# A fourth cache buffer, and the last pair's attention output read from SBUF, in one step of a hybrid decoder layer

## The chip, the cores and the metric

The kernel runs on one core of one Trainium2 chip. The metric is the device time of one execution in microseconds. Before the change it was 1331.47 us, the median of three runs from 1330.33 to 1339.6 us.

The core has TensorE (PE; its weight loads are shown as PEld), VectorE (DVE), ScalarE (ACT), GpSimd (POOL) and SyncE (SP). Here SP does nothing but issue DMAs; each engine works through its own instructions in the order in which they were placed, and so does SP: a DMA whose wait isn't over holds up all DMAs behind it.

## The reference

One layer of a decoder on 1024 prompt tokens and 8 x 8 sample tokens, all in float32, with a model width of 1024. Of the second part, the feed-forward network, only the beginning is near the change.

```
h = rms_norm(x, norm_mix_g)
a_val, a_gate, q, k, v = split(h @ w_in)                 # 256, 256, 768, 768, 768 columns
a = silu(layer_norm(depthwise_conv(a_val * sigmoid(a_gate))))
o = attend(q, k, v)                                      # 12 heads of 64
x = x + concat(a, o) @ w_out                             # 1024 x 1024
h = rms_norm(x, norm_ffn_g)
g = depthwise_conv(h @ w_ffn_gate)
x = x + (silu(g) * (h @ w_ffn_up)) @ w_ffn_down
y = rms_norm(x, norm_final_g)
```

Each of the 12 heads merges three dilated windows (128 neighbours at stride 1, 512 at 4, 2048 at 16). The sample tokens attend to their own cache (cache_k_win, cache_v_win) as well as to the new tokens.

## The kernel before

**Layout.** Prompt and sample tokens stand side by side as N = 1088 columns; channels are on the 128 partitions. Heads are worked in six pairs, one pair filling 128 partitions. Every matrix product is made from split operands: a float32 value becomes a high part (a copy by ScalarE to float32r) and a low part (a subtraction on VectorE or GpSimd), and three matmuls add high x high, high x low and low x high in PSUM.

**Stages.** First come the input projections. For pairs 0 to 2 the sample attention follows at once, in a zone of SBUF called S. In the next stage (zone P on the right) the prompt attention of earlier pairs runs beside the projections of pairs 3 to 5. Then, from about 380 us, prompt attention of the later pairs (zone P), sample attention of pairs 3 to 5 (zone U) and the output projection (operands in zone G) run together until 559 us. The output projection is cut along its inner dimension into three parts of 3, 3 and 2 tiles of 128 rows: tiles 0 and 1 are the convolution, tiles 2 to 7 the six pairs. The attention and convolution outputs travel through DRAM tensors mixed[0] to mixed[7]. The first two parts are done by out_part (matmuls at L188 to L190, evictions to x2 at L887 to L891). The last part, with mixed[6] and mixed[7], that is pairs 4 and 5, opens the next zone F and is worked in halves of 544 columns by out_half (matmuls at L942 to L945, evictions at L1165), whose result goes into the norm and on into the feed-forward products.

**The cache.** A sample attention of a pair loads four key tiles and four value tiles of 768 KB each (load_cache, L172). They rotate through SBUFS[Z][0] buffers: four in zone S, three in zone U. The scores of one chunk are made from two key tiles (L566), the outputs of one group from two value tiles (L592). The tiles of scores, turned weights and outputs (sy, spt, so) of a pair share a tag "S" with three buffers.

**The residual input.** In the second part, for each of eight row blocks, a block of the input x is loaded (xr, L882) and added to x2 by GpSimd (L883); only then may VectorE add the projection (L887). The first of these loads is issued behind a given cache load, cached[8 * NS1 + X2], that is the 23rd of the 24 cache loads of zone U.

**The last pair's way.** normalise multiplies the turned denominators into the output of a pair, in two blocks u of 512 columns (the cat tiles, L780), and stores each to mixed[2 + p] (L783). The 64 sample columns come from sample_attention (osm, L606). load_input(i, h, tag) then loads one half h of mixed[6 + i] and splits it (L1003 the load, L1006 the high part, L1007 the low part on VectorE).

**Order.** A planner places each engine's instructions from the dependences, the program's order, priorities and its own estimate of times; it is run when the kernel is built. issue_after(ins) adds only order: what its block traces on the engine of ins is placed behind ins. The loads of the last part and of the next stage are chained in this way through last_load, the high parts on ScalarE through last_high. In out_half the first eviction is placed behind lows_made[-1], the low part that was traced last:

```
earlier = rooted[0] if h and j == 1 else residuals[-1] if residuals else lows_made[-1]
with tc.issue_after(earlier):
    residuals.append(nc.vector.tensor_add(x, all_of(ps), x).ins)
```

The products of out_half rotate through four pairs of PSUM banks. The zones reuse memory: zone F begins where zone G began, and reaches over U into P, and a tile of F may be written when the tiles that lay there have been read for the last time. Weights rotate through five tiles of 4 KB (tag "W").

Of the kernel before, what the change touches and what calls it, by code (L numbers as in the profile page):

```python
# [50 lines left out]
KB, VB, QB, YB, HB, UB, PT = 4, 2, 2, 9, 8, 2, 2  # L51
DCOPY = ((2,), (2,))
AHEAD = 4000
SBUFS = {"S": (4, 3, 2), "U": (3, 3, 1)}
NS1, PN = 3, 4
HEADS = (0, 5, 8)
SHEADS = (0,10,11)
# [8 lines left out]
RING, SQS = 5, 16  # L66
FIRST = (0, 1, 2, 4, 5)
BANKS = (3, 1, 0, 2)
X2 = 22
ONACT = (0,)  # L70
HN = N // 2
HF = NF // 2
# [12 lines left out]
def trunk_kernel(tc, xT, w_in, w_first, w_out, w_gate, w_up, w_down, par, kc, vc, sa, sf, pmask, smask,  # L85
                 yT, kT, vT, ca, cas, cf):
    nc = tc.nc
    with (
# [34 lines left out]
        def zt(z, tag, bufs, s, w=N, dt=F32):  # L123
            return zone[z].tile([P, w], dt, tag=tag, name=nm(s), bufs=bufs)
# [406 lines left out]

        def sample_attention(p, Z, masks):
            mask, z = masks
            SB, PB = SBUFS[Z][1:]
            _, new, vn = spill[p]

            za, zg = z[:, :P], [z[:, (1 + g) * P:(2 + g) * P] for g in range(2)]
# [7 lines left out]
                    nc.vector.tensor_copy(zg[g][r, :].rearrange("p (j c) -> p j c", c=32)[:, :, o:o + T],  # L545
                                          src.rearrange("p (j g t) -> p g j t", g=2, t=T)[:, g])
            st = sp.tile([P, 4], F32, tag="sst", name=nm("sst"), bufs=2)
            y = zt(Z, "S", SB, "sy", 7 * P)
            nc.gpsimd.memset(y[:, NKEY:], 0.0)
            for c in range(NCH):  # L550
                ps = bank(Z, "ss", PB)
# [18 lines left out]
                                               scalar=(st[:, 0:1] if c else 3e38), accum_out=st[:, c:c + 1])  # L570
            nc.scalar.activation(y[:, :NKEY], y[:, :NKEY], AF.Exp, bias=st[:, 1:2], scale=-1.0, accum_out=st[:, 2:3])
            nc.vector.reciprocal(st[:, 3:4], st[:, 2:3])
            pT = zt(Z, "S", SB, "spt", 7 * P)
            for k0, nk in ((0, 4), (4, 3)):
                pt = bank(Z, "ss", PB)
                for k in range(nk):
                    nc.tensor.transpose(pt[:, k * P:(k + 1) * P], y[:, (k0 + k) * P:(k0 + k + 1) * P], ident)
                nc.scalar.activation(pT[:, k0 * P:(k0 + nk) * P], pt[:, :nk * P], AF.Copy)
            o2 = zt(Z, "S", SB, "so", 2 * P)
            for g in range(2):  # L580
                po = bank(Z, "ss", PB)
                tiles = [load_cache(Z, vc[p, g, c]) for c in range(NCH)]
# [185 lines left out]
        def normalise(p, den, un):  # L768
            r = exchange(den[:, 0], den[:, 1], 4)
            dn = tiny("dn", 16).rearrange("p (n k) -> p n k", k=4)  # L770
            nc.vector.tensor_add(dn, r[:, 0], den[:, 1])
            nc.vector.reciprocal(dn, dn)
            for u in range(2):
                db = zt("P", "H", HB, "db", 512).rearrange("p (k h d) -> p k h d", k=4, h=2)
                nc.vector.tensor_copy(db, dn[:, u::2].rearrange("p h k -> p k h")[:, :, :, None].to_broadcast([P, 4, 2, 64]))
                rt = bank("P", "t", PT)
                for c in range(4):
                    nc.tensor.transpose(rt[:, c * P:c * P + P], db[:, c].rearrange("p h d -> p (h d)"), ident)
                c = zt("P", "H", HB, "cat", 512)
                last_cat[0] = nc.vector.tensor_mul(c.rearrange("p (j c) -> p c j", c=4),  # L780
                                                   rt.rearrange("p (c j) -> p c j", c=4),
                                                   un[u].rearrange("p (c j) -> p c j", c=4)).ins
                nc.sync.dma_start(mixed[2 + p][:, u * 512:u * 512 + 512], c)  # L783

        before = []

        def prompt_heads(i0, i1):

# [122 lines left out]
        out_part(*part)  # L911
        for n in PARTS[1:-1]:
            out_part(*load_part(n, staged, g_part))
        zu.__exit__(None, None, None)
        zg.__exit__(None, None, None)
        zp.__exit__(None, None, None)
# [82 lines left out]
        def load_input(i, h, tag):  # L999
            nonlocal last_load, last_high  # L1000
            raw = slot("b11", "mx", F32)
            with tc.issue_after(last_load):
                last_load = nc.sync.dma_start(raw, mixed[k0 + i][:, h * HN:h * HN + HN]).ins  # L1003
            hi, lo = early[tag].pop() if early[tag] else slot(tag, "mh"), slot(tag, "ml")
            with tc.issue_after(last_high):
                last_high = nc.scalar.activation(hi, raw, AF.Copy).ins  # L1006
            lows_made.append(nc.vector.tensor_sub(lo, raw, hi.bitcast(F32)).ins)  # L1007
            part[h].append((hi, lo))

        def split_halves(t):  # L1010
# [9 lines left out]
        for h, tag in enumerate(("b11", "t2")):  # L1020
            load_input(0, h, tag)
            if not h:
                raw_wd = {m: slot("b22", "wr", F32, n1 * P) for m in ORDER[:DEFER]}
            for m0 in ORDER[h * 4:h * 4 + 4:2]:
                raw = slot("t1", "wr", F32, 2 * n * P)
                queued(raw.rearrange("p (m c) -> p m c", m=2), w_out[m0:m0 + 2, :, k0 * P:].rearrange("m p c -> p m c"))
                if m0 == ORDER[h * 4]:
                    load_input(1, h, tag)
                hi, lo = early["b21"].pop() if early["b21"] else slot("b21", "wh", w=512), slot("b21", "wl", w=512)
                with tc.issue_after(last_high):  # L1030
                    last_high = parts_of(raw, hi, lo)
                hi, lo = [t.rearrange("p (k c) -> p k c", c=P) for t in (hi, lo)]
                for j in range(2):
                    wl[m0 + j] = hi[:, j * n:j * n + n], lo[:, j * n:j * n + n]
# [6 lines left out]
        for i in range(n1):  # L1041
            hi, lo = slot("t3", "mh"), slot("t3", "ml")
            raw = lo.bitcast(F32)
            queued(raw, mixed[kd + i][:, HN:])
            with tc.issue_after(last_high):
                last_high = parts_of(raw, hi, lo)
            highs.append(last_high)
            deferred.append((hi, lo))
        for m in ORDER[:DEFER]:
            hi, lo = [slot("b22", t, w=n1 * P) for t in ("wh", "wl")]  # L1050
            with tc.issue_after(last_high):
# [701 lines left out]
```

## Time and profile before

| | |
|---|---|
| median of three runs | 1331.47 us |
| the profiled execution | 1330.07 us |
| its span | 1328.3 us |
| TensorE busy | 1291.3 us, 97% |
| VectorE, ScalarE, GpSimd busy | 941.7, 561.4, 468.9 us |
| TensorE idle, 380 to 440 us | 4.4 us |
| TensorE idle, 440 to 520 us | 6.2 us |
| HBM read and written | 153.97 MB and 56.04 MB |

The span is from the first to the last instruction of the profiled execution; its time has 1.8 us around that. A line of the profile names the engine, the line of the code (L783), the operation and the program's names as out<-in. A wait names who waited for whom. The granted clock is the share of TensorE's full clock that it was given.

### The profile page before, as it was taken

To read this page: it belongs to the slowest core of one execution; us is meant where nothing else is said; L and a number is where in the kernel's file an instruction comes from. 1 tells how busy PE (TensorE), PEld (TensorE's weight loads), DVE (VectorE), ACT (ScalarE), POOL (GpSimd) and SP (SyncE) were. 2 spreads that over 40 slices of the span, in tenths; PEclk is the share of its full clock that TensorE was granted. 3 is DMA by queue.
4 is the path that set the end of the run, shared out by engine and by line. 5 is a ranking of instruction groups with operands and counts; after the bars stand their busy time and mean duration, and the time that the engine had idled before them with its cause. 6 is when DMAs were issued, how large, how long until landed. Compare 5 with 4: busy or idle time off the path is not lost.

```text
span 1328.3 us, 25992 instructions
## 1 busy us (share of the span) xinstructions
PE 1291.3 (97%) x10322; PEld 1249.9 (94%) x10322; DVE 941.7 (71%) x1795; ACT 561.4 (42%) x1129; POOL 468.9 (35%) x384
## 2 busy tenths in 40 slices
PE   9999999999999999999999999999999999999996
PEld 9999998998978787899999999999999999999996
DVE  7479879555675666689976767667776569967656
ACT  7322121547585475355533323333233444334532
POOL 0121112111101104431765645656465535444600
PEclk9999999999999999999999999999999999999998
DMA  8247777565779879460113322133222394352412
GB/s 311 71 151 292 266 255 192 179 168 137 221 253 258 251 228 300 142 234 26 50 74 123 123 91 98 58 123 110 104 72 83 116 380 157 108 191 83 156 41 96
DMA packets 93801, 211.70 MB, mean 159 GB/s; under 512 B 13936, under 2 KB 42736, under 8 KB 93680
## 3 DMA queue, kind: packets, MB, share of 16 engines
q1 hardware_dynamic: 93392, 209.82, 48.1%
q8 instruction: 81, 1.33, 0.4%
q14 instruction: 40, 0.33, 0.1%
q10 hardware_dynamic: 288, 0.22, 0.1%
HBM read 153.97 MB, written 56.04 MB: 158 GB/s over the span
## 4 chain that ended last, share of the span: by engine, by line
PE 77%; DVE 13%; DMA 7%; issue 1%; ACT 1%; SPq 0%; DVEq 0%; ACTq 0%
PE g L188 6%; PE g L190 6%; PE g L189 6%; PE py L942 4%; PE py L944 4%; PE py L945 4%; PE g L942 4%; PE g L945 4%; PE g L944 4%; PE pz L944 3%; PE pz L942 3%; PE pz L945 3%; PE px L942 3%; PE px L945 3%; PE px L944 3%; PE o L762 3%
## 5 line engine op out<-in xcount | busy, mean ns | idle before, releaser
L188 PE MATMUL g<-xh,wh 128*128 128x384 f32 (+1 forms) x472 | 156.8, 332 | 1.6 <-DVE qkv L465 0.9
L163 POOL TENSOR_TENSOR wl<-wr,wh 128x1024 fp32r<-128x1024 f32 (+1 forms) x34 | 59.8, 1759 | 278.9 <-PE g L190 168.0
L190 PE MATMUL g<-xh,wl 128*128 128x384 f32 (+1 forms) x472 | 155.3, 329 | 0.0
L189 PE MATMUL g<-xl,wh 128*128 128x384 f32 (+1 forms) x472 | 155.2, 329 | 0.0
L942 PE MATMUL g<-ux,as 128*128 128x272 f32 x504 | 145.1, 288 | 2.3 <-DVE x L1575 1.4
L945 PE MATMUL g<-ux,as 128*128 128x272 f32 x504 | 145.4, 288 | 0.0
L944 PE MATMUL g<-ux,as 128*128 128x272 f32 x504 | 144.7, 287 | 0.0
L1093 POOL TENSOR_TENSOR wb<-wr,wb 128x512 fp32r<-128x512 f32 x79 | 116.1, 1481 | 50.2 <-ACT wb L1092 50.2
L1485 POOL TENSOR_TENSOR as<-ar,as 128x640 fp32r<-128x640 f32 (+1 forms) x56 | 89.6, 1612 | 105.9 <-ACT as L1484 105.9
L1092 ACT ACTIVATE wb<-wr 128x512 fp32r<-128x512 f32 x79 | 49.7, 629 | 162.9 <-DVE wr L1127 104.4
L942 PEld LDWEIGHTS g<-ux,as 128*128 128x128 f32 x504 | 95.0, 189 | 2.7 <-ACT as L1484 2.7
L945 PEld LDWEIGHTS g<-ux,as 128*128 128x128 f32 x504 | 94.8, 188 | 0.0
L944 PEld LDWEIGHTS g<-ux,as 128*128 128x128 f32 x504 | 94.6, 188 | 0.0
L1093 POOL TENSOR_TENSOR wa<-wr,wa 128x512 fp32r<-128x512 f32 x40 | 62.6, 1567 | 90.6 <-ACT wa L1092 86.7
L1353 DVE SCALAR_TENSOR_TENSOR fc<-gb,prm,fc 128x1104 f32<-128x1104 f32 x44 | 82.5, 1896 | 14.7 <-ACT fc L1351 14.4
L188 PEld LDWEIGHTS g<-xh,wh 128*128 128x128 f32 x472 | 88.7, 188 | 4.0 <-issue 2.0
L714 ACT ACTIVATE y<-y,m 128x128 f32<-128x128 f32 (+1 forms) x192 | 88.5, 464 | 7.9 <-DVE m L702 7.7
L189 PEld LDWEIGHTS g<-xl,wh 128*128 128x128 f32 x472 | 88.8, 188 | 0.2
L190 PEld LDWEIGHTS g<-xh,wl 128*128 128x128 f32 x472 | 88.8, 188 | 0.0
L415 DVE SCALAR_TENSOR_TENSOR cacc<-gp,prm,cacc 128x1024 f32<-128x1024 f32 x60 | 84.3, 1404 | 0.1
L677 DVE CUSTOM_DVE_ANT_0 y<-s,pmk 128x128 f32<-128x128 f32 (+1 forms) x192 | 63.6, 377 | 28.3 <-PE s L673 24.9
L161 ACT ACTIVATE wh<-wr 128x1024 fp32r<-128x1024 f32 (+1 forms) x36 | 29.6, 822 | 126.0 <-PE g L190 100.2
(390 smaller groups left out, 4297.6 us busy)
## 6 DMA issues: line engine op xcount, KB each, us to landing
cr<-in_kc SPq DMA_DIRECT2D x24, 768.0 KB, 7.5
cr<-in_vc SPq DMA_DIRECT2D x24, 768.0 KB, 7.9
ux<-ub SPq DMA_DIRECT2D x63, 272.0 KB, 4.2
kk<-dk SPq DMA_DIRECT2D x48, 256.0 KB, 6.5
wr<-in_w_in SPq DMA_DIRECT2D x20, 512.0 KB, 5.2
wr<-in_w_gate SPq DMA_DIRECT2D x20, 512.0 KB, 3.3
wr<-in_w_up SPq DMA_DIRECT2D x20, 512.0 KB, 4.7
ub<-u SPq DMA_DIRECT2D x18, 544.0 KB, 3.8
```

The lines of the kernel that those rows point to most:

```text
L188: nc.tensor.matmul(ps[c], whi[:, k, :], xh[:, t0:t0 + n], start=(k == 0), stop=False)
L189: nc.tensor.matmul(ps[c], whi[:, k, :], xl[:, t0:t0 + n], start=False, stop=False)
L190: nc.tensor.matmul(ps[c], wlo[:, k, :], xh[:, t0:t0 + n], start=False, stop=(k == nk - 1))
L415: eng.scalar_tensor_tensor(acc[:, :S], gp[:, j:j + S], col(w0 + j), acc[:, :S], op0=ALU.mult, op1=ALU.add)
L677: nc.vector.tensor_tensor_reduce(out=y[:, o:o + n], in0=ps[:, o:o + n], in1=mask, op0=ALU.add, op1=ALU.min, scale=1.0, scalar=3e38, accum_ ...
L714: nc.scalar.activation(y, y, AF.Exp, bias=m[:, 4 * g + i:4 * g + i + 1], scale=-1.0, accum_out=den[:, g, 2 * hd + u, i:i + 1])
L942: nc.tensor.matmul(ps, whi[:, k, :], xh[:, t], start=(start and k == 0), stop=False, skip_group_check=True)
L944: nc.tensor.matmul(ps, whi[:, k, :], xl[:, t], start=False, stop=False, skip_group_check=True)
L945: last = nc.tensor.matmul(ps, wlo[:, k, :], xh[:, t], start=False, stop=(stop and k == nk - 1), skip_group_check=True).ins
L1093: nc.gpsimd.tensor_sub(lo, x, hi.bitcast(F32))
L1353: nc.vector.scalar_tensor_tensor(c[:, :W], gb[i][:, t:t + W], col(C_FW + 3 * f + t), c[:, :W], op0=ALU.mult, op1=ALU.add)
L1485: nc.gpsimd.tensor_sub(lo, raw, hi.bitcast(F32))
```

## The change

Four things change.

1. In zone U the cache tiles get four buffers instead of three. In zones S and U the tiles sy, spt and so get a tag and one buffer each, instead of three shared buffers. The loads of the residual input are placed behind the 24th cache load (X2 = 23).
2. The two cat tiles of the last pair are stored through ScalarE's DMA queue instead of SP's, and kept in a list, ends.
3. After the second part of the output projection, these two tiles are split in SBUF: ScalarE makes the high parts and GpSimd the low parts of the first 544 columns, into two tiles of the weight ring (end_hi, end_lo). They take the place of the load and split of the first half of mixed[7].
4. The second half of mixed[7] is loaded and split after the deferred halves of mixed[3] to mixed[5], instead of right behind the first weights of its half. The low part of the first half of mixed[6] is made by GpSimd instead of VectorE.

```diff
--- before.py
+++ after.py
@@ -51,7 +51,7 @@
 KB, VB, QB, YB, HB, UB, PT = 4, 2, 2, 9, 8, 2, 2
 DCOPY = ((2,), (2,))
 AHEAD = 4000
-SBUFS = {"S": (4, 3, 2), "U": (3, 3, 1)}
+SBUFS = {"S": (4, 2), "U": (4, 1)}
 NS1, PN = 3, 4
 HEADS = (0, 5, 8)
 SHEADS = (0,10,11)
@@ -66,7 +66,7 @@
 RING, SQS = 5, 16
 FIRST = (0, 1, 2, 4, 5)
 BANKS = (3, 1, 0, 2)
-X2 = 22
+X2 = 23
 ONACT = (0,)
 HN = N // 2
 HF = NF // 2
@@ -531,7 +531,7 @@

         def sample_attention(p, Z, masks):
             mask, z = masks
-            SB, PB = SBUFS[Z][1:]
+            PB = SBUFS[Z][1]
             _, new, vn = spill[p]

             za, zg = z[:, :P], [z[:, (1 + g) * P:(2 + g) * P] for g in range(2)]
@@ -545,7 +545,7 @@
                     nc.vector.tensor_copy(zg[g][r, :].rearrange("p (j c) -> p j c", c=32)[:, :, o:o + T],
                                           src.rearrange("p (j g t) -> p g j t", g=2, t=T)[:, g])
             st = sp.tile([P, 4], F32, tag="sst", name=nm("sst"), bufs=2)
-            y = zt(Z, "S", SB, "sy", 7 * P)
+            y = zt(Z, "sy", 1, "sy", 7 * P)
             nc.gpsimd.memset(y[:, NKEY:], 0.0)
             for c in range(NCH):
                 ps = bank(Z, "ss", PB)
@@ -570,13 +570,13 @@
                                                scalar=(st[:, 0:1] if c else 3e38), accum_out=st[:, c:c + 1])
             nc.scalar.activation(y[:, :NKEY], y[:, :NKEY], AF.Exp, bias=st[:, 1:2], scale=-1.0, accum_out=st[:, 2:3])
             nc.vector.reciprocal(st[:, 3:4], st[:, 2:3])
-            pT = zt(Z, "S", SB, "spt", 7 * P)
+            pT = zt(Z, "spt", 1, "spt", 7 * P)
             for k0, nk in ((0, 4), (4, 3)):
                 pt = bank(Z, "ss", PB)
                 for k in range(nk):
                     nc.tensor.transpose(pt[:, k * P:(k + 1) * P], y[:, (k0 + k) * P:(k0 + k + 1) * P], ident)
                 nc.scalar.activation(pT[:, k0 * P:(k0 + nk) * P], pt[:, :nk * P], AF.Copy)
-            o2 = zt(Z, "S", SB, "so", 2 * P)
+            o2 = zt(Z, "so", 1, "so", 2 * P)
             for g in range(2):
                 po = bank(Z, "ss", PB)
                 tiles = [load_cache(Z, vc[p, g, c]) for c in range(NCH)]
@@ -780,9 +780,12 @@
                 last_cat[0] = nc.vector.tensor_mul(c.rearrange("p (j c) -> p c j", c=4),
                                                    rt.rearrange("p (c j) -> p c j", c=4),
                                                    un[u].rearrange("p (c j) -> p c j", c=4)).ins
-                nc.sync.dma_start(mixed[2 + p][:, u * 512:u * 512 + 512], c)
-
-        before = []
+                store = nc.scalar.dma_start if p == NP - 1 else nc.sync.dma_start
+                store(mixed[2 + p][:, u * 512:u * 512 + 512], c)
+                if p == NP - 1:
+                    ends.append(c)
+
+        before, ends = [], []

         def prompt_heads(i0, i1):

@@ -911,6 +914,12 @@
         out_part(*part)
         for n in PARTS[1:-1]:
             out_part(*load_part(n, staged, g_part))
+
+
+        end_hi, end_lo = [wp.tile([P, D], F32R, tag="W", name=nm(s))[:, :HN] for s in ("eh", "el")]
+        for c, (t0, n) in zip(ends, ((0, 512), (512, HN - 512))):
+            nc.scalar.activation(end_hi[:, t0:t0 + n], c[:, :n], AF.Copy)
+            nc.gpsimd.tensor_sub(end_lo[:, t0:t0 + n], c[:, :n], end_hi.bitcast(F32)[:, t0:t0 + n])
         zu.__exit__(None, None, None)
         zg.__exit__(None, None, None)
         zp.__exit__(None, None, None)
@@ -1004,7 +1013,7 @@
             hi, lo = early[tag].pop() if early[tag] else slot(tag, "mh"), slot(tag, "ml")
             with tc.issue_after(last_high):
                 last_high = nc.scalar.activation(hi, raw, AF.Copy).ins
-            lows_made.append(nc.vector.tensor_sub(lo, raw, hi.bitcast(F32)).ins)
+            lows_made.append((nc.vector if h else nc.gpsimd).tensor_sub(lo, raw, hi.bitcast(F32)).ins)
             part[h].append((hi, lo))

         def split_halves(t):
@@ -1020,12 +1029,11 @@
         for h, tag in enumerate(("b11", "t2")):
             load_input(0, h, tag)
             if not h:
+                part[0].append((end_hi, end_lo))
                 raw_wd = {m: slot("b22", "wr", F32, n1 * P) for m in ORDER[:DEFER]}
             for m0 in ORDER[h * 4:h * 4 + 4:2]:
                 raw = slot("t1", "wr", F32, 2 * n * P)
                 queued(raw.rearrange("p (m c) -> p m c", m=2), w_out[m0:m0 + 2, :, k0 * P:].rearrange("m p c -> p m c"))
-                if m0 == ORDER[h * 4]:
-                    load_input(1, h, tag)
                 hi, lo = early["b21"].pop() if early["b21"] else slot("b21", "wh", w=512), slot("b21", "wl", w=512)
                 with tc.issue_after(last_high):
                     last_high = parts_of(raw, hi, lo)
@@ -1046,6 +1054,7 @@
                 last_high = parts_of(raw, hi, lo)
             highs.append(last_high)
             deferred.append((hi, lo))
+        load_input(1, 1, "t2")
         for m in ORDER[:DEFER]:
             hi, lo = [slot("b22", t, w=n1 * P) for t in ("wh", "wl")]
             with tc.issue_after(last_high):
```

## The prediction

> **What bounds the kernel now.** I read the page first, then the matrix engine's waits, then the stretch from 380 to 620 us, the only one the diff touches.
>
> ```profile
> span 1328.3 us, 25992 instructions
> PE 1291.3 (97%) x10322; PEld 1249.9 (94%) x10322; DVE 941.7 (71%) x1795; ACT 561.4 (42%) x1129; POOL 468.9 (35%) x384
> ```
>
> TensorE is busy for 97% of the span, and no matmul or transpose is added or removed. So the change can only win TensorE's idle time (37 us in all) or matmuls that run slowly after it. The next rows show busy time by stretch: length, then PE, PEld, DVE, ACT, POOL, then granted clock, DMA share, GB/s.
>
> ```profile
> 380.00:440.00 60.00, 55.60 (x522) 48.22 (x521) 36.58 (x150) 36.95 (x112) 6.23 (x7) 1.00 0.93 281
> 440.00:520.00 80.00, 73.84 (x729) 63.83 (x728) 51.94 (x215) 49.07 (x156) 10.17 (x10) 0.98 0.86 261
> 384.00:388.00 4.00, 3.33 (x23) 2.48 (x22) 3.81 (x17) 3.98 (x18) 0.00 (x0) 1.00 1.03 419
> 500.00:512.00 12.00, 9.18 (x71) 6.70 (x67) 7.72 (x33) 4.98 (x15) 1.04 (x1) 0.86 1.05 310
> 504.00:508.00 4.00, 3.97 (x24) 2.12 (x25) 1.08 (x3) 0.70 (x1) 0.00 (x0) 0.57 1.16 278
> 560.00:564.00 4.00, 2.27 (x12) 2.24 (x13) 1.89 (x3) 2.87 (x6) 2.25 (x2) 0.80 1.00 348
> 564.00:568.00 4.00, 4.00 (x27) 4.00 (x27) 2.76 (x3) 1.74 (x4) 3.78 (x3) 0.77 1.05 392
> 576.00:620.00 44.00, 42.32 (x329) 40.90 (x328) 40.13 (x67) 25.80 (x47) 9.02 (x6) 1.00 0.25 91
> ```
>
> TensorE idles 4.4 us between 380 and 440 and 6.2 between 440 and 520. Its waits name the causes (total, times, longest):
>
> ```profile
> PE ss L566 <- DMA cr<-in_kc: 5.4, 2, 2.9
> PE s L673 <- DMA qs<-dq: 3.0, 3, 1.4
> PE g L942 <- ACT wh L993: 2.6, 1, 2.6
> PE g L945 <- POOL wl L994: 0.8, 1, 0.8
> ```
>
> and the timeline their places (start, duration, bracket: the idle time before):
>
> ```profile
> 461.68 1.50 PE L566 MATMUL ss<-cr,qz 128*32 128x384 f32 x16 [2.89 <-DMA cr<-in_kc]
> 504.03 2.49 PE L566 MATMUL ss<-cr,qz 128*32 128x384 f32 x16 [2.47 <-DMA cr<-in_kc]
> 558.83 0.31 PE L190 MATMUL g<-mh,wl 128*128 128x320 f32 x1
> 561.73 0.39 PE L942 MATMUL g<-mh,wh 128*128 128x272 f32 x1 [2.59 <-ACT wh L993]
> ```
>
> Two of the three big gaps are cache loads, one is the hand-over from the long output projection (L188 to L190) to its last part in halves (L942 to L945). After the second and the third gap the granted clock falls: at 504 to 508 us by 0.43 of 4 us (1.7 us lost), at 560 to 568 by 0.20 and 0.23 (1.7 us). After the first it doesn't.
>
> **A rule weighed: the clock.** The Trainium skill, "TensorE: Matmul & The Clock Gate", section "Why this matters for your kernels", asks for no idle gap above about 3 us between matmul bursts, so gaps of 2.5 us should leave the clock alone. Here 2.47 and 2.59 us were followed by slow matmuls and 2.89 was not, so I charge the cold stretch to the gap by the rows. By the rule the two cold stretches would stay, and the sum below would end at about 1328.8 instead.
>
> **The change, part by part.**
>
> *Fourth cache buffer.* What the queue of SP (SyncE) does around it, the first row from the chain of waits:
>
> ```profile
> 453.74 7.90 DMA cr<-in_kc
> ...
> 382.79 2.57 SPq L172 DMA_DIRECT2D cr<-in_kc  x3
> 386.82 1.09 SPq L618 DMA_DIRECT2D qs<-dq  x2
> ...
> 506.56 0.33 SPq L172 DMA_DIRECT2D cr<-in_vc  x1
> 508.40 1.05 SPq L882 DMA_DIRECT2D xr<-in_xT  x2
> ...
> 546.05 0.33 SPq L157 DMA_DIRECT2D wr<-in_w_out  x1
> 550.85 3.03 SPq L783 DMA_DIRECT2D mixed<-cat  x2
> 554.22 0.32 SPq L1003 DMA_DIRECT2D mx<-mixed  x1
> ...
> 563.99 1.61 SPq L1016 DMA_DIRECT2D ml<-mixed  x3
> ```
>
> A pair's scores need four key tiles, counted 1 to 24 with the value tiles of three pairs. With three buffers the fourth is issued only when matmuls on the first are done (453.74 for the pair that then waits at 461.68). With four it goes out beside the third, many microseconds before use, and both gaps close. That is worth 5.4 us and the cold 1.7, together 7.1 at most and 0 at least. The residual loads (L882) now follow the 24th cache load instead of the 23rd. With three buffers the 23rd waits until the 20th is read, with four the 24th does, so the release is no later, but one more tile of 128 x 1536 x 4 bytes, 786 KB, lies ahead of them. At 310 GB/s (500 to 512 us) it takes 2.5 us, and GpSimd waits for just that data:
>
> ```profile
> 517.07 7.48 POOL L883 TENSOR_TENSOR x<-x,xr 128x1088 f32<-128x1088 f32 x3 [14.95 <-DMA xr<-in_xT]
> ```
>
> Every eviction of the second projection part needs its L883. I take 7.1 - 2.5 = 4.6 us of gain.
>
> When the zone opens, three cache loads stand ahead of the q loads (382.79, 386.82), and TensorE waits up to 1.4 us for q. A fourth would stand ahead too: 786 KB at 419 GB/s is 1.9 us. Between 0 and 1.9 + 1.7 (the clock), I take 1.5 us of loss, near the row, since some of the queue drains before q. The scratch buffers cost nothing: three tiles per pair rotated through three buffers before, so each already came back to its own.
>
> *The store on ScalarE's queue and the half taken from SBUF.* SP holds the two stores from 546.4 to 554, and the loads of the last projection part stand behind them (554.22). With both stores gone, SP can issue these loads at once; their buffers lie where the attention zone kept its scores (y) and turned outputs (ot), whose last readers and writers are these (first and last start at the end of the first row):
>
> ```profile
> L741 PE MATMUL t<-ident,y x324: 270/273/421, 243.4 to 541.7; 128*128 128x128 f32 x162
> 546.92 0.59 ACT L765 ACTIVATE ot<-o 64x512 f32<-64x512 f32 x1 [1.39 <-PE o L762]
> 548.00:552.00 4.00, 4.00 (x35) 4.00 (x34) 2.81 (x7) 1.55 (x3) 1.02 (x1) 1.00 0.08 30
> ```
>
> From about 548 us they are free, and the DMA engines then stand at 8%.
>
> The removed work is one load of 272 KB, one split on ScalarE and one on VectorE. Added are two copies on ScalarE, two subtractions on GpSimd and two DMA issues on ScalarE:
>
> ```profile
> L1093 POOL TENSOR_TENSOR wb<-wr,wb 128x512 fp32r<-128x512 f32 x79 | 116.1, 1481 | 50.2 <-ACT wb L1092 50.2
> L1092 ACT ACTIVATE wb<-wr 128x512 fp32r<-128x512 f32 x79 | 49.7, 629 | 162.9 <-DVE wr L1127 104.4
> L136 ACTq DMA_DIRECT2D prm<-in_par x1: 406/406/406, 0.7 to 0.7; - x1
> ...
> 557.04 0.66 ACT L1006 ACTIVATE mh<-mx 128x544 fp32r<-128x544 f32 x1 [7.17 <-DMA mx<-mixed]
> 561.75 6.03 POOL L994 TENSOR_TENSOR wl<-wr,wh 128x512 fp32r<-128x512 f32 x4 [8.67 <-ACT wh L993]
> 564.07 1.31 DVE L1007 TENSOR_TENSOR ml<-mx,mh 128x544 fp32r<-128x544 f32 x1 [0.42 <-ACT mh L1006]
> 565.79 0.72 DVE L1165 TENSOR_TENSOR x<-g,x 128x544 f32<-128x544 f32 x1 [0.42 <-PE g L945]
> 569.63 0.72 DVE L1165 TENSOR_TENSOR x<-g,x 128x544 f32<-128x544 f32 x1 [0.52 <-PE g L945]
> ```
>
> That is 0.63 us and a narrow copy plus 2 x 0.41 on ScalarE inside its 7.17 us of idling, and 1.48 us and a narrow one on GpSimd inside 8.67: nothing, as long as the new loads' splits run before 558.8. The stores wait on ScalarE for VectorE's last product; queued behind them are the splits of the weights, for which TensorE has no use before 558.8. Without the cover the weight split would start the 1.5 us late that GpSimd's subtraction takes. The first half's split of the other tile moves from VectorE to GpSimd, in the same idle time.
>
> So the gap of 2.59, the wait of 0.8 and the cold 1.7 can go: 5.1 us. But what is late next? The second half of the last pair is now loaded after everything else, and its low part (L1007 on VectorE) is the end of the list of lows behind which the first eviction (L1165) is queued. Before, that low ran at 564.07, just ahead of the first eviction at 565.79. Now it comes last. PSUM holds four products of this part. Evictions are (569.63 - 565.79) / 3 = 1.28 us apart, so TensorE, starting at 558.9, has filled all four after 5.1 us, at 564.0, and stops until the first eviction is done.
>
> When is that? Ahead of the load in question stand the three ml loads, whose first buffer shares bytes with the last operand tile of the long projection (the zones start at the same place; the eighth slot behind 37.3 KB reaches under the 39.2 KB of operands). So SP waits there until 558.9, then issues four loads, 0.54 us each (1.61 for three), the last at about 560.5. A load took 2.8 us when few were in flight (issued 554.22, split from 557.04) and 6.2 when many were:
>
> ```profile
> DMA to landing us min/median/max: 6.1/6.2/6.2
> ```
>
> With 0.66, 0.72 and 0.72 for split, low and eviction, the fifth product starts between 565.4 and 568.8; I take a landing after 4 us, nearer the emptier row because the other loads have landed by then: 566.6. Before, the fifth product started when the fourth was evicted, 569.6. Gain 3.0, less half of a cold stretch for the new gap of 2.6 us (0.8): 2.2 us, with bounds of 4.2 and, from a landing after 6.2 and all of a cold stretch, -0.9.
>
> **The sum.** -4.6 + 1.5 - 2.2 = -5.3 us. The profiled execution took 1330.07 us (its span 1328.3 and 1.8 around it), so 1324.8 for its like; the median of the three runs is 1.4 higher, and so I forecast 1326.
>
> **The rivals.**
>
> *The first eviction waits for the piece that is loaded last, and loads do not start early.* If the planner leaves SP's order so that the loads begin at 554.2 as now, the ml loads stay near 564 less the two earlier loads, and the last one is issued at about 564.8; with 6.2 us to land and 2.1 for split, low and eviction the fifth product starts at 573.1, 3.5 us later than now, plus a cold stretch of 1.7. The other terms held, that is 1331.5 - 4.6 + 1.5 + 5.2 = 1333.6, slower than before. It decides as soon as that piece lands after 567.5 us. For it speaks that the order is written in the code, and that a store taken off SP makes no transfer faster; against it, that the DMA engines are almost empty from 548 to 552 and nothing but the two stores holds SP there. The Trainium skill, "DMA: Bandwidth & Descriptors", section "Rules for kernel authors", sides with this rival: it says that spreading DMAs over issuing engines brings no bandwidth and saves only issue time. No run here has shown yet whether that is all.
>
> *The gains are given back.* Between 576 and 620 us VectorE is busy 40.1 of 44 us, so it has little room for a TensorE that comes earlier, and GpSimd's residual additions hold the second part of the projection. Then what is left is about 1 us: 1330.5.
>
> *Everything closes.* Both cache gaps, the hand-over and their cold stretches go, and q isn't late: 12.2 us, 1319.3. A new order might also free the other idle time at 380 to 440 us, to about 1316.
>
> *The fourth buffer doesn't prefetch,* because SP is held by other waits ahead of the load: only the hand-over is won, 1329.3; I count it with the gains given back.
>
> **How the numbers follow.** Forecast (1322 to 1329) 0.50; gains given back or no prefetch 0.20; late eviction 0.13; everything closes 0.12, of which 0.05 passes 1%; something in the new order that I don't see 0.05, of which 0.02 is more than 1% faster and 0.03 more than 1% slower. The range of 1318 to 1335 takes in the full closing and the late eviction at its price and leaves out the extremes of both. A difference under 1% (13.3 us) is what a measurement of this kernel can't well tell from none. Faster than that needs more than all the gaps with their cold stretches: 0.07. Slower needs 13 us of new idling: 0.03. The rest, 0.90, lies within.
>
> **What would show it.** L566 no longer waiting for in_kc, and full clock at 500 to 512, shows the buffer right. L1003 issued near 547 instead of 554.2, and no gap between L190 and L942, shows the store right. A wait of the fifth product for L1165, with L1007 just before it, shows the new stall, and its end (566.6 or 573) decides between forecast and first rival. A longer wait of L673 for qs at 398 would show the loss at the opening. The forecast is wrong if the stretch from 440 to 520 still idles by 6 us, or if a new wait appears in the attention that none of these rows shows.

## The result, and the profile after

After the change the kernel takes 1338.28 us (median of 20 runs, 1333.47 to 1344.34), beside 1331.59 us before in the same comparison. The ratio is 1.005, with a 95% interval of 1.0036 to 1.0063: 0.5% slower, where 0.4% faster was forecast, and outside the range of 1318 to 1335. The profiled execution has a span of 1335.1 us, 6.8 more than before. The engines' busy times on the page of the changed kernel:

```profile
PE 1293.8 (97%) x10322; PEld 1253.4 (94%) x10322; DVE 936.4 (70%) x1793; ACT 561.0 (42%) x1130; POOL 472.5 (35%) x387
```

TensorE idles 41.3 us instead of 37.0, and its same 10322 matmuls take 2.5 us longer. Lines behind the changed places have moved in the code: L942, L944 and L945 are now L951, L953 and L954, L1165 is L1174, L1003, L1006 and L1016 are L1012, L1015 and L1025, L887 is L890, and L922 makes the low part el. Busy time by stretch in the changed kernel, columns as before (length, PE, PEld, DVE, ACT, POOL, granted clock, DMA share, GB/s):

```profile
380.00:440.00 60.00, 56.00 (x523) 47.72 (x520) 36.80 (x144) 34.65 (x106) 5.26 (x6) 0.97 1.02 316
440.00:520.00 80.00, 76.23 (x764) 67.98 (x763) 56.66 (x191) 45.88 (x140) 25.20 (x17) 0.98 0.90 274
500.00:512.00 12.00, 10.15 (x114) 9.28 (x115) 10.24 (x29) 4.47 (x16) 11.69 (x7) 0.86 0.71 195
540.00:560.00 20.00, 17.03 (x140) 15.66 (x139) 9.95 (x22) 9.51 (x26) 2.51 (x3) 1.00 0.30 99
560.00:580.00 20.00, 11.81 (x61) 11.30 (x62) 7.08 (x9) 11.18 (x22) 14.81 (x13) 0.69 0.78 261
620.00:640.00 20.00, 17.49 (x124) 17.09 (x125) 19.73 (x29) 12.01 (x23) 5.28 (x3) 0.91 0.00 1
```

The same view of the kernel before, where the prediction hadn't shown it:

```profile
540.00:560.00 20.00, 19.14 (x148) 18.47 (x146) 10.27 (x19) 5.16 (x9) 3.75 (x4) 1.00 0.37 110
560.00:580.00 20.00, 17.49 (x124) 17.24 (x125) 14.08 (x17) 13.37 (x25) 14.91 (x10) 0.91 1.01 370
620.00:640.00 20.00, 19.97 (x159) 19.75 (x158) 20.00 (x32) 11.59 (x20) 6.50 (x2) 1.00 0.00 1
```

TensorE's idle time from 440 to 520 us did fall, from 6.2 to 3.8 us. The clock from 500 to 512 us is 0.86 as before, not full as forecast. The idle time rose from 0.9 to 3.0 in the last 20 us of the attention, and from 2.5 to 8.2 in the 20 us after, where the clock fell to 0.69 as well. TensorE's waits from 380 to 620 us (total, times, longest) and their places (start, duration, bracket: the idle time before):

```profile
PE g L951 <- DVE x L1174: 5.9, 1, 5.9
PE s L673 <- DVE st L677: 4.1, 2, 3.7
PE g L951 <- ACT wh L1002: 2.9, 1, 2.9
PE o L762 <- DMA vw<-dv: 2.4, 1, 2.4
PE t L778 <- DVE db L775: 2.3, 1, 2.3
```

```profile
558.71 0.63 PE L778 MATMUL t<-ident,db 128*128 128x128 f32 x4 [2.31 <-DVE db L775]
562.21 0.82 PE L951 MATMUL g<-mh,wh 128*128 128x272 f32 x2 [2.87 <-ACT wh L1002]
576.98 0.57 PE L951 MATMUL g<-mh,wh 128*128 128x272 f32 x1 [5.90 <-DVE x L1174]
620.89 0.79 PE L237 MATMUL g<-ident,rr 128*128 128x128 f32 x5 [1.46 <-DVE rr L225]
632.04 0.40 PE L972 MATMUL pv<-b22l,wa 128*128 128x272 f32 x1 [1.62 <-DVE b22l L1078]
```

The waits of L566 for in_kc are gone, but four others stand in their place (the longest of L673 for st ends at 501.80 us), and the last part of the projection starts at 562.21 us, 0.5 later than before (561.73), behind a gap of 2.87 us instead of 2.59. The largest new wait is the one of the fifth product for the first eviction.

How far this goes: the first matmul of px on b21h in the feed-forward network started at 656.4 us before (L942) and starts at 667.5 now (L951). So 10.6 us are lost between the start of the last part and there. From the stretches: 5.7 of idle time and about 2.1 of slow clock (0.31 x 11.81 less 0.09 x 17.49) from 560 to 580, 2.5 of idle time and 1.6 of slow clock from 620 to 640; that is 11.9, a rough sum, since a stretch has one mean clock and some of its idle time lies ahead of the start. Of the 11.1 us that are missing at this matmul, 4.3 come back by the end (the spans differ by 6.8); I didn't follow where.

**Why the eviction is late.** SP's issues in the changed kernel, and what SP waited for from 540 to 575 us:

```profile
556.45 7.46 SPq L1025 DMA_DIRECT2D wr<-in_w_out  x5
563.96 1.85 SPq L1025 DMA_DIRECT2D wr<-in_w_gate  x4
565.85 1.66 SPq L1025 DMA_DIRECT2D ml<-mixed  x3
567.55 1.10 SPq L1012 DMA_DIRECT2D mx<-mixed  x1
```

```profile
SPq L1025 <- PE t L741: 10.7, 1, 10.7
SPq L1025 <- DMA mixed<-cat: 5.3, 2, 3.9
```

ScalarE and VectorE at the end of the same chain:

```profile
560.48 0.33 ACTq L784 DMA_DIRECT2D mixed<-cat  x1
560.86 0.23 ACT L921 ACTIVATE eh<-cat 128x32 fp32r<-128x32 f32 x1 [1.49 <-DVE cat L780]
561.00 0.64 ACT L1015 ACTIVATE mh<-mx 128x544 fp32r<-128x544 f32 x1
561.54 1.13 ACT L1002 ACTIVATE wh<-wr 128x512 fp32r<-128x512 f32 x2
...
572.26 2.04 ACT L1002 ACTIVATE mh<-ml 128x544 fp32r<-128x544 f32 x3 [7.84 <-DMA ml<-mixed]
574.30 0.66 ACT L1015 ACTIVATE mh<-mx 128x544 fp32r<-128x544 f32 x1
```

```profile
574.99 1.21 DVE L1016 TENSOR_TENSOR ml<-mx,mh 128x544 fp32r<-128x544 f32 x1 [10.11 <-ACT mh L1015]
576.12 2.60 DVE L1174 TENSOR_TENSOR x<-g,x 128x544 f32<-128x544 f32 x4
```

The piece that is loaded last is issued at 567.55 us, 7 us later than forecast, and split only at 574.30, behind the three mh<-ml splits that had to wait for their own loads until 572.26. Its low part (574.99) and the first eviction (576.12) follow at once; VectorE had idled 10 us, and evicts four products in a row.

SP stood in two places. One is the wait for the prompt attention's last transposes (L741), whose tiles lay where the weights go. The other is a wait for the store of cat, though that store is no longer on SP. In the built program, though in no view of the profile, the DMAs of SP and ScalarE take turns at eight completion semaphores, and two of the five w_out loads take those of the two stores: they must see them finished first. The stores on GpSimd's queue, below, test this.

**Why the cover is gone.** The last start of three groups: long projection (L190), last products of the attention (L780), and the attention's scores (L673). Before:

```profile
L190 PE MATMUL g<-mh,wl x135: 283/337/429, 392.5 to 558.8; 128*128 128x384 f32 x78, 128*128 128x320 f32 x39, 128*128 128x272 f32 x18
L780 DVE TENSOR_TENSOR cat<-t,un x12: 1047/1084/1098, 295.4 to 552.4; 128x512 f32<-128x512 f32 x12
L673 PE MATMUL s<-kk,qw x192: 222/283/388, 219.9 to 517.2; 128*128 128x256 f32 x168, 128*128 128x128 f32 x24
```

After:

```profile
L190 PE MATMUL g<-mh,wl x135: 283/337/468, 391.1 to 553.6; 128*128 128x384 f32 x78, 128*128 128x320 f32 x39, 128*128 128x272 f32 x18
L780 DVE TENSOR_TENSOR cat<-t,un x12: 1058/1083/1106, 294.5 to 559.4; 128x512 f32<-128x512 f32 x12
L673 PE MATMUL s<-kk,qw x192: 222/284/582, 217.5 to 533.8; 128*128 128x256 f32 x168, 128*128 128x128 f32 x24
```

Before, the long projection runs on for 6 us after the last cat product; in program order 45 of its matmuls stand behind the transposes of that product. After, it ends 6 us ahead of it, and none stand there. With four buffers the planner places the sample attention earlier (its last scores, L566, start at 485.4 instead of 505.7 us) and the last pair's scores 17 us later, and fills TensorE meanwhile with the projection, which is then used up.

### The profile page after: what moved, and what is told of

It is laid out like the page before. It is cut to its first block, busy times and chain, and to the rows that moved or that the text cites. A ratio compares the mean times of both kernels' runs of the same rounds, so it can differ in the third digit from the quotient of the medians.

```text
span 1335.1 us, 26004 instructions
## 1 busy us (share of the span) xinstructions
PE 1293.8 (97%) x10322; PEld 1253.4 (94%) x10322; DVE 936.4 (70%) x1793; ACT 561.0 (42%) x1130; POOL 472.5 (35%) x387
## 4 chain that ended last, share of the span: by engine, by line
PE 83%; DVE 10%; DMA 4%; issue 2%; ACT 0%; SPq 0%; DVEq 0%; ACTq 0%
PE g L188 6%; PE g L190 6%; PE g L189 6%; PE g L951 5%; PE g L954 5%; PE g L953 5%; PE py L951 5%; PE py L953 5%; PE py L954 4%; PE px L954 3%; PE pz L953 3%; PE pz L951 3%; PE pz L954 3%; PE px L953 3%; PE px L951 3%; PE s L673 3%
## 5 line engine op out<-in xcount | busy, mean ns | idle before, releaser
L190 PE MATMUL g<-xh,wl 128*128 128x384 f32 (+1 forms) x472 | 155.4, 329 | 0.0
L951 PE MATMUL g<-ux,as 128*128 128x272 f32 x504 | 145.2, 288 | 0.4 <-DVE x L1584 0.4
L954 PE MATMUL g<-ux,as 128*128 128x272 f32 x504 | 145.4, 289 | 0.0
L953 PE MATMUL g<-ux,as 128*128 128x272 f32 x504 | 144.8, 287 | 0.0
L951 PEld LDWEIGHTS g<-ux,as 128*128 128x128 f32 x504 | 95.1, 189 | 0.8 <-issue 0.8
L954 PEld LDWEIGHTS g<-ux,as 128*128 128x128 f32 x504 | 94.9, 188 | 0.0
L953 PEld LDWEIGHTS g<-ux,as 128*128 128x128 f32 x504 | 94.7, 188 | 0.0
L190 PEld LDWEIGHTS g<-xh,wl 128*128 128x128 f32 x472 | 88.9, 188 | 0.0
L1102 POOL TENSOR_TENSOR wa<-wr,wa 128x512 fp32r<-128x512 f32 x40 | 54.6, 1366 | 79.4 <-ACT wa L1101 79.4
```

Source lines behind the costliest of these rows:

```text
L190: nc.tensor.matmul(ps[c], wlo[:, k, :], xh[:, t0:t0 + n], start=False, stop=(k == nk - 1))
L951: nc.tensor.matmul(ps, whi[:, k, :], xh[:, t], start=(start and k == 0), stop=False, skip_group_check=True)
L953: nc.tensor.matmul(ps, whi[:, k, :], xl[:, t], start=False, stop=False, skip_group_check=True)
L954: last = nc.tensor.matmul(ps, wlo[:, k, :], xh[:, t], start=False, stop=(stop and k == nk - 1), skip_group_check=True).ins
L1102: nc.gpsimd.tensor_sub(lo, x, hi.bitcast(F32))
```

## The experiments

All times are medians, each with the ratio to the kernel before on the same chip; the ratio is not the quotient of the two medians and can differ from it by 0.1%.

| kernel | us | ratio (95%) |
|---|---|---|
| the change | 1338.28 | 1.005 (1.0036 to 1.0063) |
| four buffers alone | 1337.04 | 1.0053 (1.0034 to 1.0073) |
| the change with three buffers | 1330.96 | 1.0009 (0.9994 to 1.0025) |
| the change, first eviction freed | 1331.73 | 0.9999 (0.9982 to 1.0015) |
| the change, last load put back | 1332.37 | 1.0004 (0.9985 to 1.0023) |
| three buffers, eviction freed | 1327.19 | 0.9986 (0.996 to 1.0013) |
| the same, timed again | 1326.72 | 0.9962 (0.9941 to 0.9982) |
| four buffers, eviction freed, projection kept back | 1328.53 | 0.9984 (0.9968 to 1.0) |
| late last load alone | 1336.07 | 1.0040 (1.0024 to 1.0055) |
| three buffers, eviction freed, stores on SP | 1330.29 | 1.0 (0.9981 to 1.002) |
| three buffers, stores on GpSimd | 1329.29 | 0.9977 (0.9948 to 1.0005) |
| three buffers, eviction freed, stores on GpSimd | 1327.77 | 0.998 (0.9954 to 1.0006) |

### Four buffers alone

The kernel before, with the change's first point and nothing else:

```diff
-SBUFS = {"S": (4, 3, 2), "U": (3, 3, 1)}
+SBUFS = {"S": (4, 2), "U": (4, 1)}
-X2 = 22
+X2 = 23
```

> Only the four cache buffers, the separate scratch tags and the later residual loads; the last pair's way is that of before. Theory A (the loss lies in the last part of the output projection: its first eviction stands behind the low part of the piece that is loaded last): the buffers by themselves cost nothing, 1326 to 1333 us; the two waits of L566 for in_kc are gone, and what they gave is partly lost where the last pair's attention ends later than its filler work. Theory B (the loss comes from the new order that four buffers give the attention, with its filler used up too early): 1335 to 1340 us.

By the ratios it costs as much as the whole change, by the medians 5.5 us beside 6.7. The two waits for in_kc are not both gone here, as they are in the whole change: one is left. That wait, and the hand-over in TensorE's order of time:

```profile
PE ss L566 <- DMA cr<-in_kc: 2.7, 1, 2.7
```

```profile
571.86 0.60 PE L942 MATMUL g<-mh,wh 128*128 128x272 f32 x1 [8.64 <-ACT wh L993]
```

With no projection left to run, the whole way from the last cat product over store, load and splits lies open, 8.6 us. The fourth buffer isn't free, and this is its price where the store is unchanged.

### The change with three buffers

```diff
-SBUFS = {"S": (4, 2), "U": (4, 1)}
+SBUFS = {"S": (4, 2), "U": (3, 1)}
-X2 = 23
+X2 = 22
```

> The changed kernel with three cache buffers and the residual loads behind the 23rd cache load as before. Theory A: the fifth product of the last part still waits for its eviction, 4 to 7 us and matmuls at a low clock after it: 1335 to 1340 us. Theory B: 1326 to 1331 us.

TensorE reaches the last part with a gap of 0.68 us only: with the projection left as cover, the half from SBUF closes the hand-over as forecast. But the time is that of before: the stall of the first theory came with the time of the second. TensorE's fifth product, and SP's issues and wait:

```profile
572.47 0.37 PE L951 MATMUL g<-mh,wh 128*128 128x272 f32 x1 [4.82 <-DVE x L1174]
```

```profile
551.26 7.83 SPq L1025 DMA_DIRECT2D wr<-in_w_out  x5
...
562.66 0.48 SPq L1012 DMA_DIRECT2D mx<-mixed  x1
```

```profile
SPq L1025 <- DMA mixed<-cat: 5.7, 2, 5.5
```

What the closed gap gives, the late eviction takes back, and SP is again held by the stores that had left its queue.

### The first eviction freed

The change, with the first half's first eviction behind the second low part instead of the last one:

```diff
-                earlier = rooted[0] if h and j == 1 else residuals[-1] if residuals else lows_made[-1]
+                earlier = rooted[0] if h and j == 1 else residuals[-1] if residuals else lows_made[-1 if h else 1]
```

> The changed kernel, in which the first eviction of the first half is placed behind the low part of mixed[6]'s second half instead of that of mixed[7]'s second half, which is loaded last; nothing else is moved, and up to the last part the instructions stand in the same order as in the changed kernel. Theory A: the stall of 5.9 us at the fifth product and most of the slow clock around it go, 1328 to 1333 us. Theory B: the stall's cause is elsewhere (the loads themselves, or the attention's late end), at most 2 us better than the changed kernel: 1336 to 1338 us.

The wait of 5.9 us is gone, the first eviction runs at 568.18 us, right behind the product that it evicts, and 6.6 us come back.

### The last load put back, and the late last load alone

Two opposite edits on the same line. In the change, the second half of mixed[7] loaded again behind the first weights of its half:

```diff
+                if h and m0 == ORDER[4]:
+                    load_input(1, 1, "t2")
...
-        load_input(1, 1, "t2")
```

> The changed kernel with the second half of mixed[7] loaded and split where the kernel before had it, behind the first weights of its half; the first eviction stays behind its low part. Theory A: that low part is early again, the stall goes, and the time is within 2 us of the run with the eviction freed, 1328 to 1333 us. If moving the load is not what made the low late (SP held by the buffers under the attention's last tiles), the stall stays at 4 us or more: 1334 to 1338 us.

In the kernel before, only that load moved behind the deferred halves:

```diff
-                if m0 == ORDER[h * 4]:
+                if not h and m0 == ORDER[0]:
                     load_input(1, h, tag)
...
+        load_input(1, 1, "t2")
```

> The kernel before, in which only the load and split of mixed[7]'s second half are moved behind the deferred halves; buffers, stores and the first half's load as before. Theory C: the first eviction waits for it, 5 to 8 us at the fifth product: 1335 to 1340 us. If the hand-over's own wait covers it, 1331 to 1333 us.

Putting it back returns 5.9 us, no stall at the fifth product. Moving it alone costs 4.5, with a wait of 4.5 us there. So the late load is a cost by itself, with either number of buffers. The second loss goes with it: this kernel has the waits of L237 (1.5 us) and of pv for b22l (2.2) between 580 and 660 us that the changed one has, and the kernels with the load put back or the eviction freed don't. But the change with three buffers has neither wait, though its fifth product stands for 4.82 us, so the late eviction alone does not explain them; what else they need is left open here.

### Three buffers and the eviction freed, with its stores on each queue

Both edits together:

> Three cache buffers and residual loads behind the 23rd cache load, the last pair's way as in the changed kernel, and the first eviction no longer behind the low part of the piece loaded last. Theory C (two separate costs: four buffers leave no matmuls of the projection to cover the end of the last pair's attention; the late low part stops the first eviction): both are gone, and of the 4.8 us stall of the run with three buffers at least 3 us come back: 1325 to 1328 us. If the eviction's wait was only covering another one (the second half's operands), it stays at 1330 to 1332 us.

No wait above 1.6 us is left between 540 and 600 us, and the clock is 1.00 from 560 to 580. The first timing can't tell the gain from none; it was repeated:

> The fastest version so far (three cache buffers, first eviction freed, stores on ScalarE's queue) timed a second time, beside the kernel before and beside the version with the stores on GpSimd's queue. If its gain is real, the ratio lies again at 0.998 to 0.999 (1327 us), and the interval of the two together excludes 1; if it was chance, it lies at 1.000.

The second interval excludes 1: 0.4% faster, 4.8 us by the medians. Of the kernels here it is the fastest, and the only one that is shown to beat the kernel before; the changed one is some 11 us slower by the medians. What the store's queue gives in it:

```diff
-                store = nc.scalar.dma_start if p == NP - 1 else nc.sync.dma_start
+                store = nc.sync.dma_start
```

> As the run with three buffers and the freed eviction, with the last pair's two stores back on SP's queue; the first half is still taken from SBUF. If the store's queue matters because SP stands in line for VectorE's product, the loads of the last part start 5 us later again, near 554 us, and the hand-over waits 2 to 4 us: 1328 to 1332 us. If only the half taken from SBUF matters, the same as that run within 1 us.

With the stores on SP it is some 3 us slower, with a clock of 0.65 from 576 to 580 us around waits of TensorE for split weights (L1002 1.1, L1003 0.8 us; they end from 575.05 to 577.37). The loads of the last part start later, as forecast (the first at 556.02 instead of 548.24 us); the waits of 2 to 4 us at the hand-over itself did not come, its gap is 0.7 us in both. The intervals of the two times overlap, so this size is rough.

### The projection kept back

The change with the eviction freed, and the last two row blocks of the long projection placed behind the last transposes of the attention:

```diff
-                gemm(w, part, n, ev, chunks=CHUNKS if k0 == 0 or m not in ORDER[:DEFER] else HALF)
+                with tc.issue_after(last_turn[0]) if k0 and m > 5 else nullcontext():
+                    gemm(w, part, n, ev, chunks=CHUNKS if k0 == 0 or m not in ORDER[:DEFER] else HALF)
```

> Four buffers, eviction freed, and the last two row blocks of the long output projection (45 matmuls, the number that stands there with three buffers) placed behind the last pair's turned denominators. Theory C, strict (missing cover at the hand-over is the whole cost of the four buffers): the gap of 2.9 us and the slow clock after it go: 1324 to 1328 us. Rival (the cover is only moved: the chain of the last attention before it now idles by as much): 1330 to 1334 us, with the idle time at 540 to 558 us instead.

The gap at the hand-over falls from 2.87 to 0.68 us, and the time by 3.2 to 1328.5, between the two forecasts. That shows the lost cover as the cause of that gap. But TensorE now lacks these matmuls ahead of it: from 540 to 560 us it is busy for 16.04 of 20 us, as the rival had it; with the eviction freed alone it was 17.68. Four buffers with the cover restored aren't shown to be better than three.

### The stores on GpSimd's queue

The wait of SP for a store that ScalarE issues was read from the trace and the built program. This takes it away in the kernel with three buffers; the orders of TensorE, VectorE and SP stay the same, instruction for instruction:

```diff
-                store = nc.scalar.dma_start if p == NP - 1 else nc.sync.dma_start
+                store = nc.gpsimd.dma_start if p == NP - 1 else nc.sync.dma_start
```

> Three cache buffers, everything else as changed, but the last pair's two stores go out on GpSimd's queue instead of ScalarE's; the order of TensorE, VectorE and SP is that of the run with three buffers, instruction for instruction. Theory (SP is held from 551.3 to 559.1 us because its later loads take the completion semaphores of the two stores on ScalarE's queue, which they must see finished first): SP's loads no longer wait for mixed<-cat, the five w_out loads that took 7.83 us take about 2, the gate loads go out by 555 instead of 559.15, the last half of the last tile is issued by 560.5 instead of 562.66, the stall of 4.82 us at the fifth product shrinks to 3 or less, and the time falls by 1.5 to 3 us, to 1328 to 1329.5. Rival (SP waits there for data or for buffers, whoever stores): the block of 7.8 us stays, the stall stays at 4.8, the time stays at 1331.

The wait for mixed<-cat falls from 5.7 to 0.3 us and the five loads take 2.39 us instead of 7.83. The stall at the fifth product is 2.2 us instead of 4.82, and the median 1329.3, as expected; the runs spread over 1319 to 1338 us, so the gain of 1.7 isn't shown by the times alone. In the profiled execution all of this stands some 5 us later, after idle time and a clock of 0.83 from 520 to 540 us, ahead of the stores; its cause is not shown. The same edit with the eviction freed stands at the same time as its counterpart:

> Three cache buffers, the first eviction freed from the low that comes last, and the two stores on GpSimd's queue; its order is otherwise that of the fastest version so far. Theory: the loads of the last part land 3 us earlier, but no product waits for them there any more, so the time stays within 1 us of that version's, 1326.5 to 1327.5. Rival: the remaining waits of 1 to 3 us behind the hand-over hang on these loads too, and the time falls to 1325; or GpSimd, which then issues two stores ahead of the second half's low parts, delays those by more than 1 us and the time rises to 1329.

SP's issues there with the stores on ScalarE's queue, and then on GpSimd's, with SP's wait:

```profile
551.50 7.69 SPq L1025 DMA_DIRECT2D wr<-in_w_out  x5
559.25 1.84 SPq L1025 DMA_DIRECT2D wr<-in_w_gate  x4
...
562.57 0.60 SPq L1012 DMA_DIRECT2D mx<-mixed  x1
```

```profile
551.35 2.40 SPq L1025 DMA_DIRECT2D wr<-in_w_out  x5
553.83 3.13 SPq L1025 DMA_DIRECT2D wr<-in_w_gate  x4
559.77 1.40 SPq L1025 DMA_DIRECT2D ml<-mixed  x3
561.46 0.32 SPq L1012 DMA_DIRECT2D mx<-mixed  x1
```

```profile
SPq L1025 <- PE g L190: 2.4, 1, 2.4
```

The block shrinks from 7.69 to 2.40 us with nothing moved but the store, so SP was held by the store's completion and not by data or buffers. The weights go out 5.4 us earlier, the last piece only 1.1 (3 were expected): ml then waits for the last operand of the long projection, just the wait for which the forecast had SP stand still until 558.9. The time is that of the kernel with ScalarE's queue, since there no product waits for these loads.

## Why the prediction was wrong

**The fourth buffer, forecast at -4.6 and +1.5 us.** The prefetch worked: L566 no longer waits in the changed kernel (alone, the buffers left 2.7 of the 5.4 us). But the forecast took everything else as it stood. The 2.4 us that TensorE idles less from 440 to 520 us are spent again on 2.1 more from 540 to 560 and on a clock of 0.97 from 380 to 440, 1.8 us, so that the last part starts 0.5 us later than before, not 3.1 earlier. The step that failed is that closing both gaps is "worth 5.4 us and the cold 1.7": it counted closed idle time as time won, while the matmuls that fill it are the projection's, taken from the end, where they covered the last pair's attention, and that attention ended 7 us later (L780 at 559.4 instead of 552.4). Nor did the cold 1.7 go: 500 to 512 us is at 0.86 before and after, now behind a wait of 3.7 us of L673 for st, a new wait in the attention of the kind that the forecast had named as a sign against it. Alone the buffers cost 5.5 us (the scratch tags with them; these had no run of their own). No later start of L673 for qs showed, which was the loss that I had charged at the opening; what came there is a wait of 2.4 us for vw.

**ScalarE and GpSimd, forecast at nothing "as long as the new loads' splits run before 558.8".** I had named the cover, the long projection, and hadn't asked whether the first edit takes it. It does. The first split stands at 561.00 us behind the second store and its copy (560.48, 560.86), though its data was there, and TensorE starts at 562.21. Splits placed ahead of the stores on ScalarE were not tried; for the loads on SP that wait for the stores, the engines would wait for one another in that order.

**"With both stores gone, SP can issue these loads at once."** This is the step of the second term (-2.2) that failed, and the stores on GpSimd's queue show why: the store had gone from SP, but not the wait for its completion. The five loads took 7.5 us, the last piece went out at 567.55 instead of 560.5 (562.66 with three buffers, so 5 us of it come from the later attention). With three buffers the term as a whole measured nothing in place of -2.2 (1330.96 beside 1331.51, ratio 1.0009).

**"I take a landing after 4 us."** In the kernel with three buffers it was split 7.1 us after its issue, behind the three splits of ml; and it was 6.7 in the changed one. With the stores on GpSimd's queue, where the split waited for nothing but this load, it was 5.0 (566.81 to 571.84). Here only a size was off, and the bound of 6.2 too: "nearer the emptier row because the other loads have landed by then" doesn't hold where they go out at 559 to 562.

**The first rival** was right in mechanism: the first eviction waited behind the low of the piece loaded last, and the fifth product stood. Its price of +5.2 us at the fifth product compares with 6.6 us for freeing the eviction. Added to the sum with the buffers' gain it gave 1333.6 us; without that gain, which didn't exist, it would have been 1336.7. I gave it 0.13 because "nothing but the two stores holds SP there", true of before and no argument on what the stores would do elsewhere. By the Trainium skill, "DMA: Bandwidth & Descriptors", section "Rules for kernel authors", another issuing engine brings no bandwidth and saves only issue time. No run here measures bandwidth by queue; what was saved is that SP no longer stands for VectorE's product, while SP's rows show that the wait for the store's completion stayed with it.

**What held.** The direction of the hand-over where its cover is there (gap 0.68 instead of 2.59 us). And the last pair's way did win once the first eviction no longer waited: it gives, by the medians, 4.4 and 4.8 us with three buffers (the scratch tags included, and the first interval still takes in no gain), and 5.3 with four (1331.73 beside 1337.04). That a difference under 1% can't well be told from none did not hold: the interval of the change excludes 1 at 0.5%.

**The clock is undecided.** I had charged slow clock to gaps of 2.5 us against the rule on gaps of the Trainium skill, "TensorE: Matmul & The Clock Gate", section "Why this matters for your kernels" (none above about 3 us). The changed kernel is on the rows' side: its wait of 2.4 us for vw, at 412 us, makes the 0.97 from 380 to 440, and after 2.31 and 2.87 us at the hand-over the clock is 0.58 and 0.57 from 560 to 568. With the projection kept back the same 2.31 us, at 556.38, is followed by 1.00. So my charge is no rule either.

## What to carry to other kernels

An idle gap that is closed with work from the same list opens again where that work was the cover: before counting a gain, look which matmuls will fill the gap and what they hide now. A list whose last element others are queued behind (here lows_made[-1]) must be read again whenever something is appended later. And a DMA moved to another engine's queue takes its issue away, but not its completion, if the queues share semaphores: look in the trace whether the first engine still waits for it.

## What was not expected of the hardware

SP waited 5.0 to 5.7 us for the completion of stores that ScalarE had issued, and 0.2 to 0.3 with the stores on GpSimd's queue. GpSimd takes 0.56 to 0.71 us to issue one (L784), about twice the 0.33 us of ScalarE (560.48 above), and that cost no time which these runs can tell.

Slow clock came without a gap of even 1 us, too. In the kernel with the last load put back it is 0.58 from 392 to 396 us; the 4 us before are busy for 2.63, and the longest single gap of the 10 us before is 0.94 us (by stretch, and on TensorE in order of time):

```profile
388.00:392.00 4.00, 2.63 (x16) 2.00 (x16) 3.86 (x22) 4.00 (x15) 0.00 (x0) 1.00 1.03 421
392.00:396.00 4.00, 3.96 (x28) 3.90 (x30) 3.96 (x8) 2.46 (x3) 0.00 (x0) 0.58 1.01 418
```

```profile
392.04 0.62 PE L188 MATMUL g<-mh,wh 128*128 128x384 f32 x2 [0.94 <-ACT mh L279]
```

The changed kernel passes the same place from 384 to 388 us, busy for 2.62 of 4 with a longest gap of 0.95, and keeps 1.00. And one kernel differs from itself: with three buffers and the eviction freed, a wait of 1.32 us that ends at 582.77 was followed by 1.00 from 584 to 588 us in the first profile, and one of 1.06, ending at 581.76, by 0.68 in the second.

So neither the rule nor my charge by the length of one gap says when the clock falls; what decides it is left open here.
